# A hybrid encoder layer: the Hyena half of the output projection and the second norm, ordered by hand

## The chip, the cores and the metric

The kernel runs on one core of one Trainium2 chip. The metric is the time of one execution on the device in microseconds, the median of several runs; lower is better. The engines are PE (matmuls and transposes), DVE and POOL (element-wise work), ACT (element-wise work with functions, casts and copies) and SP, which here only issues DMAs; ACT can issue DMAs too.

## The reference

One encoder layer on 2048 positions of width 1024, in fp32. The left half of the projection's columns feeds an attention, the right half a Hyena operator (long convolutions by FFT, each followed by a gate); each half is RMS-normed by itself, both go through one output projection, and the sum with x is normed again ahead of a squared-ReLU MLP.

```python
def hyena_mixer(u, conv_w, conv_b, w1, ..., deltas, skip_d):
    uc = short_conv(u, conv_w, conv_b)
    v, x1, x2 = jnp.split(uc, HY_ORDER + 1, axis=-1)
    taps_f = hyena_filters_freq(seq_len, w1, b1, w2, b2, w3, b3, w4, freq, deltas)
    zz = v.astype(jnp.float32)
    gates = (x1, x2)
    for n in range(HY_ORDER):
        conv = fft_long_conv(zz, taps_f[:, n]) + skip_d[n].astype(jnp.float32) * zz
        zz = gates[n].astype(jnp.float32) * conv
    return zz.astype(u.dtype)

        mix = jnp.concatenate([rms_norm(att, attn_out_g[i]), rms_norm(hy, hy_out_g[i])], axis=-1)
        h = h + mix @ w_out[i]
        m = rms_norm(h, norm2_g[i])
        h = h + jnp.square(jax.nn.relu(m @ w_mlp_in[i])) @ w_mlp_out[i]
    return rms_norm(h, final_g)
```

## The kernel before, in words

**Precision.** An fp32 product is made of three matmuls (`mm3`, L162 to L164): both operands are split into a rounded part and a rest (hi and lo, type fp32r), and hi·hi, hi·lo and lo·hi are summed in one PSUM bank.

**Stages**, in microseconds from the start of the profiled span: the projection (0 to 230), attention with the Hyena inputs beside it (230 to 1226), the filters' transform (`filter_dft`, 1240 to 1415), the two convolutions (`conv` with o = 0 from 1420 and o = 1 from 1575), the rest of the output projection and the second norm (`mix`, 1719 to 1910), then the MLP's first and second matrix.

**Convolution's end.** The last loop of `conv` has 16 blocks of 32 channels. For each, PE transposes 8 tiles (bt, L1470), ACT copies them out of PSUM (b, L1471, two copies), PE makes 4 matmuls (yo, L1488), ACT copies one half of the result (odd, L1490), DVE adds and subtracts it (L1491, L1492), POOL multiplies by the gate (L1493), and SP writes the block to DRAM (z_d). The copies for a block stand ahead of the block before on PE and ACT (`turned(gb + 1)`).

**Attention half of the projection.** `att_part` is a generator: each step takes one chunk of 128 rows (three matmuls op of 128x512); eight steps make one tile of 128 positions, and h goes to h_d. Its steps are pumped between the steps of `filter_dft` and `conv` by the counts PUMP_F and PUMP_C; what is left runs at the start of `mix`.

**Mix.** For 16 tiles, in the order 0, 4, 1, 5, ... of each half: `hy_operands` loads 128 positions of z_d (mx), ACT casts hi (L622) and DVE subtracts lo (L623), ACT squares it (sq, L650), PE sums the squares over the channels (ss, L653), and DVE and ACT make the norm's factor (ar). `project` makes 24 matmuls (op) and DVE adds the result to h (L665). `normed` squares h on ACT with an accumulated sum (L730), makes the factor in small steps (r2, L112 to L119), and DVE writes m (L732). `turn` transposes the tile before (mt, L744, 8 transposes), and ACT scales the result into sa or sb (L746). After every second tile come four subtractions for the MLP's Strassen form (L705 to L707, L751), and `keep` splits seven operands of 128x512 (L759, L760), or in the second half writes them to mo_d. In `mlp_in`, two products run early ahead of the last tile's transposes (g), and the third (p = 6) needs sums of the weights' quarters (L697 to L699) and their split (wop, L819).

**What sets the order.** `filter_dft` and `conv` run under `in_order`: each engine takes its instructions as the code writes them. `mix` and the MLP are placed by the scheduler of the framework.

Of the kernel before, what the change touches and what calls it, by code (L numbers as in the profile page):

```python
# [45 lines left out]
def setup(tc, ctx, a):  # L46
# [19 lines left out]
    k.z_d = [k.dram.tile([HYW, SEQ], F32, name=f"z_d{i}") for i in range(2)]  # L66
# [537 lines left out]
def mix_setup(k, pool):  # L604
    nc, a = k.nc, k.a
    k.go = k.wa.tile([P, 8], F32, name="go")
    nc.scalar.dma_start(out=k.go[:, 0:4], in_=a["attn_out_g"][0].rearrange("(c p) -> p c", p=P),
                        allow_slow_non_contiguous=True)
    nc.scalar.dma_start(out=k.go[:, 4:8], in_=a["hy_out_g"][0].rearrange("(c p) -> p c", p=P),
                        allow_slow_non_contiguous=True)  # L610
    nc.vector.tensor_mul(out=k.go[:, 4:8], in0=k.go[:, 4:8], in1=k.norm[:])
    k.norm2 = k.wa.tile([P, 4], F32, name="norm2")
    aligned(k.wa, 64)
    nc.vector.tensor_mul(out=k.norm2[:], in0=k.norm[:], in1=k.norm[:])
    k.weights = mix_weights(k, pool, 0)
    next(k.weights)
# [28 lines left out]
def hy_operands(k, ps, t):  # L645
    nc = k.nc
    hx = k.wa.tile([P, 4, P], F32, name="mx", bufs=2)
    nc.sync.dma_start(out=hx[:], in_=k.z_d[1][:, t * P:(t + 1) * P].rearrange("(c p) t -> p c t", p=P))
    sq = k.wa.tile([P, 4, P], F32, name="sq")
    nc.scalar.activation(out=sq[:], in_=hx[:], func=AF.Square)  # L650
    sp = ps.get("s", "ss")
    for c in range(4):
        nc.tensor.matmul(sp[:, 0:1], sq[:, c], k.norm2[:, c:c + 1], start=c == 0, stop=c == 3)  # L653
    r = rstd_from_root(k, k.wa, sp[:, 0:1], QW, 1, "ar")
    return (*operand_parts(k, hx[:]), r)
# [57 lines left out]
def mix(k, mo, pool, ps, side, mlp):  # L713
# [7 lines left out]
    weights = mix_weights(k, mo, 1)  # L721
    next(weights)
    pump(side, 10 ** 6)
    hx = hy_operands(k, ps, tiles[0])
    *_, wo = weights

    def normed(h):
        m = mo.tile([P, DM], F32, name="m", tag="raw", bufs=NRAW)
        ssq = pool.tile([P, 1], F32, name="r2s", bufs=2)
        nc.scalar.activation(out=m[:], in_=h[:], func=AF.Square, accum_out=ssq[:])  # L730
        r2 = rstd_from_root(k, pool, ssq[:], DM, 1, "r2")
        nc.vector.tensor_scalar_mul(out=m[:], in0=h[:], scalar1=r2[:])  # L732
        return m

    def turn(half, i, s, m):
        if s == 0:
            k.sa = pool.tile([P, 2, 4, P], F32, name="sa", bufs=2)
        else:
            k.sb = pool.tile([P, 5, 4, P], F32, name="sb", bufs=1)
        b = k.sb if s else k.sa  # L740
        for c in range(2):
            tp = ps.get("s", "mt")
            for d in range(4):
                nc.tensor.transpose(tp[:, d * P:(d + 1) * P], m[:, (4 * c + d) * P:(4 * c + d + 1) * P], k.ident[:])  # L744
            for d in range(4):
                nc.scalar.mul(out=b[:, c, d], in_=tp[:, d * P:(d + 1) * P], mul=g2[:, 4 * c + d:4 * c + d + 1])  # L746
        if s:
            sa, sb = k.sa, k.sb
            engine = nc.gpsimd if half and i == 3 else nc.vector
            right_sums(engine, sb[:, 2], sb[:, 3], sb[:, 0], sa[:, 0], sb[:, 0], sb[:, 1])  # L750
            engine.tensor_sub(out=sb[:, 4], in0=sa[:, 1], in1=sb[:, 3])  # L751
            return half, slice(i * P, (i + 1) * P), [sa[:, 0], sa[:, 1]] + [sb[:, j] for j in range(5)]

    def keep(half, cs, ops):
        for j, x in enumerate(ops):
            if half:
                nc.sync.dma_start(out=k.mo_d[j, :, :, cs], in_=x)
                continue
            nc.scalar.copy(out=k.mh[j][:, :, cs], in_=x)  # L759
            (nc.gpsimd if j in MIX_POOL else nc.vector).tensor_sub(out=k.ml[j][:, :, cs], in0=x,  # L760
                                                                   in1=f32(k.mh[j][:, :, cs]))

    late, done = [], None
    for n, t in enumerate(tiles):
        h = pool.tile([P, DM], F32, name="h", bufs=2)
        nc.sync.dma_start(out=h[:], in_=k.h_d[t * P:(t + 1) * P, :])
        if n == NT - 2:
            next(mlp)
        cur = hx
        if n + 1 < NT:  # L770
            hx = hy_operands(k, ps, tiles[n + 1])
        for j in range(2):
            pump(project(k, ps, j, h[:, j * 512:(j + 1) * 512], wo, *cur), 10)
        nc.sync.dma_start(out=k.h2_d[t * P:(t + 1) * P, :], in_=h[:])
        due, done = done, None
        if len(late) == ML:
            done = turn(*late.pop(0))
        late.append((*order[n], normed(h)))
        if due:
            keep(*due)  # L780
    next(mlp)
    for x in late:
        done = turn(*x)
    keep(*done)


ML = 1
# [4 lines left out]
def mlp_in(k, mo, ps):  # L792
# [14 lines left out]
    def prepare(n, p):  # L807
        if p == 1:
            if n == 0:
                load(1)  # L810
# [361 lines left out]
def filter_taps(k, f1, ps):  # L1172
# [52 lines left out]
    nc.vector.reciprocal(out=k.norm[:], in_=k.norm[:])  # L1225

# [120 lines left out]
def filter_dft(k, g1, ps, side):  # L1347
# [6 lines left out]
    for o in range(2):  # L1354
# [13 lines left out]
        else:  # L1368
            k.feed.close()
            k.feed = Feed(k, "ux", a["dft_data"], [k.u_d[0:HYW], k.z_d[0]], (gps,), FEED_C, 16)  # L1370
# [22 lines left out]
PUMP_F = 6, 1  # L1393
FB = 6
FOLD_C = 8
PUMP_C = 4, 1, 3, 0


def conv(k, o, c1, ps, side):
    nc, a = k.nc, k.a  # L1400
    gate = blocks(k.u_d[(o + 1) * HYW:(o + 2) * HYW])
    dst = blocks(k.z_d[o])
# [72 lines left out]
    nc.sync.dma_start(out=d4[:], in_=a["idft"])  # L1475
    nxt = turned(0)
    for gb in range(16):
# [3 lines left out]
        pump(side, PUMP_C[3] * (gb % 2))  # L1481
# [3 lines left out]
        yo = ps.get("x", "yo")[:, 0].rearrange("p (q g m) -> p q g m", q=2, m=HF)  # L1485
        for q in range(2):
            for half in range(2):
                nc.tensor.matmul(yo[:, q], d4[:, q, half], cur[:, half, q], start=half == 0, stop=half == 1)  # L1488
        odd = c1.tile([P, 2, HYW], F32, name="odd", tag="t2", bufs=2)[:, 0, :4 * HF].rearrange("p (g m) -> p g m", m=HF)
# [4 lines left out]
        nc.sync.dma_start(out=dst[:, 4 * gb:4 * gb + 4], in_=gx)  # L1494
        if o == 0:
            k.feed.limit += 1
            k.feed.fill(gb >= FOLD_C)

# [94 lines left out]
def encoder_layer(tc, a):  # L1593
    with ExitStack() as ctx:
# [10 lines left out]
        with sbuf(k, "wa") as k.wa:  # L1605
            with sbuf(k, "hp") as hp, Banks(k, "ps3", {"s": 4}, {"x": 2}) as ps:
                side = att_part(k, hp, ps, list(range(NT)))
                with sbuf(k, "fd") as fd:
                    mix_setup(k, fd)
                    with in_order(tc):  # L1610
                        filter_dft(k, fd, ps, side)
                with sbuf(k, "cv") as cv, in_order(tc):
                    conv(k, 0, cv, ps, side)
                    conv(k, 1, cv, ps, side)
                k.feed.close()
                with sbuf(k, "mo") as mo:
                    mlp = mlp_in(k, mo, ps)
                    with sbuf(k, "mx") as mx:
                        mix(k, mo, mx, ps, side, mlp)
# [22 lines left out]
```

## Time and profile before

| | us |
|---|---|
| median of three runs | 3161.52 (3160.85 to 3162.79) |
| the profiled execution's own time | 3162.0 |
| its span, first to last instruction | 3160.1 |
| PE busy | 2997.1 (95%) |
| DVE busy | 2053.7 (65%) |
| POOL busy | 1683.2 (53%) |
| ACT busy | 1427.0 (45%) |
| mean granted TensorE clock | 0.974 of full speed |

A row of a window gives the length, then the busy time of each engine with its instructions, the granted clock of PE, the share of the DMA engines that is busy, and GB/s. A row of the waits names the waiting engine and instruction, what released it, the total, the number and the longest. In a timeline a row begins with its start and its duration; brackets give the idle time ahead of it.

### The profile page before, as it was taken

Reading aid. Unit: us, or ns where it says so; the run is one execution under the profiler, and the core shown is the slowest. Engines: PE = TensorE matmul, PEld = TensorE weight load, DVE = VectorE, ACT = ScalarE, POOL = GpSimd, SP = SyncE. Lnnn points to the kernel's source line nnn. Section 1 sums busy time; section 2 is a strip of 40 time slices with the busy share of each in tenths; the row PEclk is TensorE's granted clock in tenths of the full one; section 3 lists DMA queues with packets and bytes.
Section 4 is the critical chain, followed back from the end, with each engine's and each line's share of the span. In section 5 each row is a group of like instructions: output and inputs, shape, how many; then the busy total and the mean of one; then the engine's idle time right before and its main releaser. Section 6 shows DMA issues by size and latency. Waiting matters only on the chain.

```text
span 3160.1 us, 40370 instructions
## 1 busy us (share of the span) xinstructions
PE 2997.1 (95%) x13400; PEld 2258.8 (71%) x13400; DVE 2053.7 (65%) x3197; ACT 1427.0 (45%) x2641; POOL 1683.2 (53%) x1339
## 2 busy tenths in 40 slices
PE   7977999999999998999999888999999989999998
PEld 6754666666666666665757777888788878888887
DVE  7987776666665555777473667777977644454455
ACT  7865655555554444553434553333333233223333
POOL 3434777778778786335553116777877544250010
PEclk9988999999999999999999889999999999999999
DMA  7758344334423425776755455445544395433454
GB/s 224 222 153 235 113 128 143 110 108 136 140 101 121 153 77 173 262 253 192 206 160 181 134 183 182 152 150 176 201 165 155 120 326 173 133 116 128 143 184 153
DMA packets 477581, 518.67 MB, mean 164 GB/s; under 512 B 39604, under 2 KB 346292, under 8 KB 470332
## 3 DMA queue, kind: packets, MB, share of 16 engines
q1 hardware_dynamic: 472460, 512.11, 50.3%
q10 hardware_dynamic: 4912, 3.97, 0.5%
q8 instruction: 107, 1.75, 0.2%
q14 instruction: 102, 0.84, 0.1%
HBM read 321.99 MB, written 193.99 MB: 163 GB/s over the span
## 4 chain that ended last, share of the span: by engine, by line
PE 77%; DVE 6%; DMA 3%; POOL 2%; issue 2%; ACT 1%; SPq 0%; POOLq 0%; ACTq 0%; DVEq 0%
PE o L500 6%; PE y L163 6%; PE y L164 6%; PE y L162 6%; PE g L164 5%; PE g L163 5%; PE g L162 5%; PE st L479 4%; PE X L1335 3%; PE st L480 3%; PE sc L459 3%; PE uo L162 3%; PE uo L163 3%; PE uo L164 3%; PE yo L1488 2%
## 5 line engine op out<-in xcount | busy, mean ns | idle before, releaser
L487 POOL TENSOR_TENSOR sum<-sum,p 128x512 f32<-128x512 f32 x416 | 553.4, 1330 | 127.7 <-ACT p L482 101.7
L462 DVE TENSOR_REDUCE top<-sc 128x1 f32<-128x512 f32 x512 | 347.2, 686 | 260.2 <-PE sc L459 257.5
L482 ACT ACTIVATE p<-st 128x512 f32<-128x512 f32 x512 | 303.8, 598 | 310.4 <-PE st L480 295.4
L162 PE MATMUL g<-mh,wop 128*128 128x512 f32 x896 | 349.9, 391 | 6.8 <-ACT wop L819 6.8
L163 PE MATMUL g<-ml,wop 128*128 128x512 f32 x896 | 349.8, 390 | 4.2 <-DVE ml L830 4.2
L164 PE MATMUL g<-mh,wop 128*128 128x512 f32 x896 | 349.7, 390 | 0.4 <-DVE wop L820 0.4
L162 PE MATMUL y<-bh,ah 128*128 128x512 f32 x768 | 299.5, 390 | 7.8 <-ACT bh L987 7.8
L163 PE MATMUL y<-bh,ah 128*128 128x512 f32 x768 | 299.4, 390 | 0.9 <-DVE bh L988 0.9
L996 DVE TENSOR_TENSOR ah<-ar,ah 128x1024 fp32r<-128x1024 f32 x111 | 149.8, 1350 | 230.8 <-ACT ah L995 230.6
L164 PE MATMUL y<-bh,ah 128*128 128x512 f32 x768 | 299.3, 390 | 0.0
L995 ACT CAST ah<-ar 128x1024 fp32r<-128x1024 f32 x111 | 117.1, 1055 | 344.1 <-PE y L164 333.7
L500 PE MATMUL o<-p,vt 128*64 128x512 f32 x1024 | 234.9, 599 | 0.0
L459 PE MATMUL sc<-kt,q 128*128 128x512 f32 x512 | 208.0, 411 | 13.4 <-DVE top L462 11.3
L479 PE MATMUL st<-q,kt 128*128 128x512 f32 x512 | 214.7, 419 | 1.3 <-ACT p L482 1.2
L480 PE MATMUL st<-q,kt 128*128 128x512 f32 x512 | 203.1, 397 | 0.0
L162 PEld LDWEIGHTS g<-mh,wop 128*128 128x128 f32 x896 | 168.9, 189 | 42.1 <-ACT wop L819 7.0
L163 PEld LDWEIGHTS g<-ml,wop 128*128 128x128 f32 x896 | 168.8, 188 | 40.5 <-DVE ml L830 5.4
L164 PEld LDWEIGHTS g<-mh,wop 128*128 128x128 f32 x896 | 168.8, 188 | 36.2 <-DVE wop L820 1.1
L819 ACT CAST wop<-ws 128x512 fp32r<-128x512 f32 x128 | 79.2, 621 | 221.4 <-PE g L164 192.0
L162 PEld LDWEIGHTS y<-bh,ah 128*128 128x128 f32 x768 | 144.4, 188 | 38.4 <-ACT bh L987 8.4
L163 PEld LDWEIGHTS y<-bh,ah 128*128 128x128 f32 x768 | 144.5, 188 | 31.3 <-DVE bh L988 1.4
L164 PEld LDWEIGHTS y<-bh,ah 128*128 128x128 f32 x768 | 144.5, 188 | 29.9
(290 smaller groups left out, 7053.4 us busy)
## 6 DMA issues: line engine op xcount, KB each, us to landing
ar<-H_d SPq DMA_DIRECT2D x111, 512.0 KB, 3.9
uw<-uw_d SPq DMA_DIRECT2D x36, 1024.0 KB, 4.9
w1raw<-in_w_mlp_in SPq DMA_DIRECT2D x64, 512.0 KB, 4.1
H_d<-r SPq DMA_DIRECT2D x96, 256.0 KB, 2.2
H_d<-s SPq DMA_DIRECT2D x96, 256.0 KB, 2.0
F_d<-F SPq DMA_DIRECT2D x34, 512.0 KB, 2.8
F<-F_d SPq DMA_DIRECT2D x34, 512.0 KB, 4.1
aT<-aT_d SPq DMA_DIRECT2D x32, 512.0 KB, 6.1
```

Of the source, the lines that this page charges most:

```text
L162: mm(out, l_hi, r_hi, start=start, stop=False)
L163: mm(out, l_hi, r_lo, start=False, stop=False)
L164: mm(out, l_lo, r_hi, start=False, stop=stop)
L459: nc.tensor.matmul(s[:], u.q[:, h], kt[u.kv, b][0][:], start=True, stop=True)
L462: nc.vector.tensor_reduce(out=u.top[:, h, b:b + 1], in_=s[:], axis=AX.X, op=ALU.max, negate=True)
L479: nc.tensor.matmul(s[:], lo[:, c], u.q2[:].rearrange("p h t -> p (h t)"), start=True, stop=False)
L480: nc.tensor.matmul(s[:], hi[:, c], u.q[:].rearrange("p h t -> p (h t)"), start=False, stop=True)
L482: nc.scalar.activation(out=p[:], in_=s[:], func=AF.Exp)
L487: nc.gpsimd.tensor_add(out=u.sum[:], in0=u.p0[:] if j == 1 else u.sum[:], in1=p[:])
L500: nc.tensor.matmul(u.o[cols], vt[j // 8][:, j % 8, u.kv], p[:], start=j < 2, stop=j > 13)
L995: nc.scalar.copy(out=h[:, 0], in_=raw[:])
L996: nc.vector.tensor_sub(out=h[:, 1], in0=raw[:], in1=f32(h[:, 0]))
```

## The change

- **Attention half.** More steps are pumped (PUMP_F from 6, 1 to 6, 2; PUMP_C's last from 0 to 1, and in convolution 1 alone), and what is left at block 10 of convolution 1's last loop is run there. `mix` starts without any.
- **Hyena's norm.** While convolution 1's blocks leave, ACT squares them and PE sums them over channels by four matmuls with a selector sel (ssq_add); a table n2 of 512 factors is loaded for it by eight DMAs, and sel is made on DVE. The factor hr of all tiles is made once, at the end.
- **Hyena's parts.** hi and lo are made there too (POOL copies, DVE subtracts) and written to DRAM apart (zp_d); `hy_load` reads them. The weights' lower half wo is split there at blocks 11 to 14.
- **Mix by hand.** `mix` runs under `in_order`. Tile by tile: 24 products of one tile, then the transposes of the tile before; its norm runs under these products. The four subtractions and seven splits become a list of jobs, taken out one and five at a time.
- **Loads.** h has three buffers and is loaded two tiles ahead; the second load of the MLP's weights moves from p = 1 to p = 6.

```diff
+def hy_load(k, n, t):
+
+    first = n < 2
+    parts = []
+    for i in range(2):
+        name = "mx" if n % 3 == 2 else ("oh", "ol")[i]
+        p = k.wa.tile([P, 4, P], F32R, name=name, bufs=2)
+        src = k.zp_d[i, :, t * P:(t + 1) * P].rearrange("(c p) t -> p c t", p=P)
+        for c in range(4 if first else 1):
+            cs = slice(c, c + 1) if first else slice(0, 4)
+            k.nc.sync.dma_start(out=f32(p[:, cs]), in_=src[:, cs])
...
+    def added(u, j):
+        js = slice(j * 512, (j + 1) * 512)
+        nc.vector.scalar_tensor_tensor(out=u.h[:, js], in0=u.d[j][:], scalar=hr[:, u.t:u.t + 1], in1=u.h[:, js],
+                                       op0=ALU.mult, op1=ALU.add)
+
+    def squared(u, j):
+        js = slice(j * 512, (j + 1) * 512)
+        nc.scalar.activation(out=u.m[:, js], in_=u.h[:, js], func=AF.Square, scale=DM ** -0.5,
+                             accum_out=u.ssq[:, j:j + 1])
...
+    def normed(u):
+        nc.sync.dma_start(out=k.h2_d[u.t * P:(u.t + 1) * P, :], in_=u.h[:])
+        y, r, e = (pool.tile([P, 1], F32, name=f"r2{x}", bufs=2) for x in "yre")
+        nc.vector.tensor_scalar(out=y[:], in0=u.ssq[:, 0:1], scalar1=u.ssq[:, 1:2], scalar2=EPS,
+                                op0=ALU.add, op1=ALU.add)
+        nc.scalar.activation(out=e[:], in_=y[:], func=AF.Sqrt)
...
+        for j in range(2):
+            js = slice(j * 512, (j + 1) * 512)
+            nc.vector.tensor_scalar_mul(out=u.m[:, js], in0=u.h[:, js], scalar1=r[:])
...
+        for j in (4, 0, 5, 1, 6, 2, 3):
+            jobs.append(lambda j=j: keep(j))
...
+    for n in range(NT):
+        u = queue.pop(0)
+        if n + 2 < NT:
+            queue.append(load(n + 2))
...
+        if n == 0:
+            v = queue[0]
+            for w in (u, v):
+                for j in range(2):
+                    products(w, j, (0, 1, 2))
+            for j in range(2):
+                products(u, j, (3,))
...
+        if old:
+            added(old, 1)
+            squared(old, 1)
+            work(1)
+            normed(old)
+            if older:
+                taken(older)
+            turned(old)
+        room(u)
+        if n < NT - 1:
+            added(u, 0)
+            squared(u, 0)
+            work(5)
+        older, old = old, u
...
-PUMP_F = 6, 1
+PUMP_F = 6, 2
...
-PUMP_C = 4, 1, 3, 0
+PUMP_C = 4, 1, 3, 1
...
+def hy_sums(k, cz):
+
+    nc = k.nc
+    n2 = cz.tile([P, HYW // 8], F32, name="n2")
+    src = k.n2_d.rearrange("(g c) -> c g", c=8)
+    for c in range(8):
+        nc.scalar.dma_start(out=n2[c * NT:(c + 1) * NT], in_=src[c:c + 1].to_broadcast([NT, HYW // 8]),
+                            allow_slow_non_contiguous=True)
...
+    nc.vector.tensor_mul(out=sel[:], in0=mask[:].unsqueeze(1).to_broadcast([P, HYW // 8, NT]),
+                         in1=n2[:].unsqueeze(2).to_broadcast([P, HYW // 8, NT]))
...
+    def ssq_add(to, gb, z2):
+        for g in range(4):
+            nc.tensor.matmul(to[:, :NT], z2[:, g], sel[:, 4 * gb + g], start=g == 0, stop=g == 3)
+        nc.vector.tensor_add(out=k.hssq[:], in0=to[:, :NT], in1=k.hssq[:])
...
-        pump(side, PUMP_C[3] * (gb % 2))
+        if o and gb < 11:
+            pump(side, 10 ** 6 if gb == 10 else PUMP_C[3])
...
         nc.gpsimd.tensor_mul(out=gx, in0=y, in1=gx)
-        nc.sync.dma_start(out=dst[:, 4 * gb:4 * gb + 4], in_=gx)
...
+        nc.scalar.activation(out=y, in_=gx, func=AF.Square)
+        squares.append((gb, y))
+        hl = cz.tile([P, 2, 4, P], F32R, name="zp", bufs=2)
+        nc.gpsimd.tensor_copy(out=hl[:, 0], in_=gx)
+        nc.vector.tensor_sub(out=hl[:, 1], in0=gx, in1=f32(hl[:, 0]))
+        for i in range(2):
+            nc.sync.dma_start(out=dst[i][:, 4 * gb:4 * gb + 4], in_=f32(hl[:, i]))
+        if gb > 10:
+            k.wo1 = next(weights, None) or k.wo1
```

Three places show what the change does to the order. The first is ACT at the end of convolution 1, before: b are the copies out of PSUM for the next block, odd is the half of this block's result that DVE waits for.

```order
L1471 COPY b<-bt 128x512 x2
L1490 COPY odd<-yo 128x256
L1471 COPY b<-bt 128x512 x2
L1490 COPY odd<-yo 128x256
L1471 COPY b<-bt 128x512 x2
```

The same place after the change, from ACT's last copies of the inverse transform (L1532) to the second block; n is the table n2, L1616 is the square of a finished block.

```order
L1532 COPY A<-b 128x128x4 x20
L1487 DMA n_15338<-n_d 16x64x1 x8
L593 DMA oraw<-in_w_out 128x1024 x4
L1570 COPY b<-bt 128x512 x4
L1607 COPY odd<-yo 128x256
L1616 ACTIVATE both<-both 128x512
L1570 COPY b<-bt 128x512 x2
L1607 COPY odd<-yo 128x256
L1616 ACTIVATE both<-both 128x512
L1570 COPY b<-bt 128x512 x2
```

Between one block's odd and the next one's now stands the square of the first, with the copies behind it, and twelve DMA issues stand ahead of the first copies. The second place is DVE in `mix`'s first half after the change, from the step in which a pair of tiles is complete to the next; L805 to L808 are the four subtractions, L802 the rest of a split, L745 the addition to h, L760 to L769 the norm.

```order
L745 SCALAR_TENSOR_TENSOR h<-op,hr,h 128x512
L805 TENSOR_TENSOR sb<-sb,sa 128x512
L806 TENSOR_TENSOR sb<-sb 128x512
L807 TENSOR_TENSOR sb<-sb 128x512
L808 TENSOR_TENSOR sb<-sa,sb 128x512
L745 SCALAR_TENSOR_TENSOR h<-op,hr,h 128x512
L802 TENSOR_TENSOR ml_15983<-sa,mh_15976 128x4x128
L760 TENSOR_SCALAR r2y<-r2s 128x1
L763 RECIPROCAL r2r<-r2e 128x1
L764 TENSOR_TENSOR r2e<-r2r 128x1
```

The subtractions and splits of the pair before stand between the two halves of a tile's addition and ahead of its norm. The third place is ACT in the same step.

```order
L788 ACTIVATE sb<-mt,g_15974 128x128 x8
L750 ACTIVATE m,r2s<-h 128x512
L801 CAST mh_15980<-sb 128x4x128
L750 ACTIVATE m,r2s<-h 128x512
L801 CAST mh_15976<-sa 128x4x128
L762 ACTIVATE r2e<-r2y 128x1
L788 ACTIVATE sa<-mt,g_15974 128x128 x8
L750 ACTIVATE m,r2s<-h 128x512
L801 CAST mh_15981<-sb 128x4x128
L801 CAST mh_15977<-sa 128x4x128
```

The first cast of a pair (L801) reads what the first of the four subtractions on DVE wrote, and the square of the next half of h (L750) and the root for the norm (L762) queue behind it.

204 lines of the change are left out of this document (123 added, 81 removed).

## The prediction

> **What bounds the kernel now.** I read the chain that ended last first, then windows over the stretch that is rebuilt, then PE's waits in it.
>
> ```profile
> PE 77%; DVE 6%; DMA 3%; POOL 2%; issue 2%; ACT 1%; SPq 0%; POOLq 0%; ACTq 0%; DVEq 0%
> ```
>
> PE sets the end over three quarters of the span, so a stage is worth what PE idles or works in it. The windows: convolution 1's last loop, the attention half left over, `mix`'s first and second half, the step to the MLP's third product; then the filters' second loop and the rest of convolution 1.
>
> ```profile
> 1676.80:1718.80 42.00, 41.94 (x260) 37.66 (x258) 12.55 (x35) 24.09 (x51) 17.75 (x14) 1.00 0.55 160
> 1718.80:1747.00 28.20, 23.42 (x97) 18.38 (x96) 9.91 (x22) 5.02 (x9) 2.58 (x2) 0.88 0.71 225
> 1747.00:1862.00 115.00, 95.89 (x435) 80.01 (x434) 75.55 (x189) 63.72 (x169) 19.20 (x12) 0.85 0.39 127
> 1862.00:1903.10 41.10, 37.06 (x200) 30.70 (x199) 27.24 (x81) 23.74 (x72) 0.00 (x0) 1.00 0.89 271
> 1903.10:1916.60 13.50, 6.72 (x36) 5.45 (x34) 6.29 (x10) 5.45 (x19) 5.87 (x4) 0.84 0.72 210
> ...
> 1372.00:1415.00 43.00, 42.57 (x136) 24.94 (x137) 30.40 (x54) 22.17 (x31) 2.82 (x4) 1.00 0.82 297
> 1575.00:1676.80 101.80, 99.08 (x310) 58.53 (x311) 67.68 (x91) 36.45 (x79) 56.55 (x54) 0.97 0.53 165
> ```
>
> The first five make 239.8 us; everything of size in the change falls into them. The loop at the top is PE's (41.94 of 42.00); `mix`'s first half loses 19 us idle, and its clock is 0.85. PE's waits from 1718 to 1920:
>
> ```profile
> PE mt L744 <- DVE r2y L112: 17.7, 4, 4.4
> PE g L162 <- ACT wop L819: 6.8, 1, 6.8
> PE mt L744 <- DVE m L732: 4.7, 4, 2.0
> ```
>
> The transposes mt wait for the second norm, 22.4 us in all; the new order puts products over them. The idle time costs again, through the clock:
>
> ```profile
> 1781.84 1.19 PE L744 MATMUL mt<-ident,m 128*128 128x128 f32 x8 [4.40 <-DVE r2y L112]
> ...
> 1785.39 0.63 PE L164 MATMUL op<-wo,ol 128*128 128x512 f32 x1
> ...
> 1790.74 0.39 PE L164 MATMUL op<-wo,ol 128*128 128x512 f32 x1
> ```
>
> After 4.40 us of idling the matmuls last 0.63 us; five microseconds later 0.39 again, so some 0.2 us less each. The pace at full clock, from two early products (24 matmuls between the first row's end and the last), with the transposes and the old norm's sums:
>
> ```profile
> 1769.89 1.06 PE L744 MATMUL mt<-ident,m 128*128 128x128 f32 x8 [0.68 <-DVE m L732]
> 1770.80 0.95 PE L653 MATMUL ss<-norm,sq 128*128 128x1 f32 x8
> 1771.61 0.48 PE L162 MATMUL op<-wo,oh 128*128 128x512 f32 x1
> ...
> 1902.29 1.07 PE L744 MATMUL mt<-ident,m 128*128 128x128 f32 x8 [1.96 <-DVE m L732]
> 1903.11 0.48 PE L162 MATMUL g<-mh,wop 128*128 128x512 f32 x1
> ...
> 1908.69 1.03 PE L744 MATMUL mt<-ident,m 128*128 128x128 f32 x8
> ```
>
> 1903.11 to 1908.69 is 5.58 us, 0.2325 a matmul; eight transposes take 0.91 and 0.82, so 0.87; ss takes 0.81.
>
> **Part 1, attention half.** The second window's matmuls are 29 steps of three; 29 x 3 x 0.2325 = 20.2 us. They go to places where PE has no room (42.57 of 43.00, 99.08 of 101.80), so they are paid in full there, with some transposes 20.5. The 28.2 us go. Their DMAs (512 KB of h in and out a tile) join a window at 297 GB/s and share 0.82, in which each step also lengthens the loop by 0.7 us; I take nothing for them, bound 3.
>
> **Part 2, convolution 1's last loop.** One block of before:
>
> ```profile
> 1696.67 0.37 ACT L1490 COPY odd<-yo 128x256 f32<-128x256 f32 x1 [1.08 <-issue]
> 1697.11 1.07 ACT L1471 COPY b<-bt 128x512 f32<-128x512 f32 x2
> 1697.13 0.42 DVE L1491 TENSOR_TENSOR both<-yo,odd 128x256 f32<-128x256 f32 x1 [1.83 <-POOL both L1493]
> ...
> 1698.02 1.27 POOL L1493 TENSOR_TENSOR both<-both 128x512 f32<-128x512 f32 x1 [1.32 <-DVE both L1492]
> ...
> 1699.27 0.37 ACT L1490 COPY odd<-yo 128x256 f32<-128x256 f32 x1 [1.08 <-issue]
> ```
>
> The period is 2.60 us, and ACT runs ahead: its copies follow odd at once. In the new order the square of this block stands ahead of those copies. So odd (1696.67) to POOL's end (1699.29) is 2.62 us, then the square, then the copies, then the next odd: a closed loop. A square of 128x512 is 0.64 us, in the groups of `mix`:
>
> ```profile
> L760 POOL TENSOR_TENSOR ml<-sb,mh 128x512 fp32r<-128x512 f32 x12 | 19.2, 1626 | 109.1 <-DVE are L117 55.3 <-DMA mx<-z_d 53.8
> ...
> L650 ACT ACTIVATE sq<-mx 128x512 f32<-128x512 f32 x15 | 9.7, 643 | 0.9 <-PE ss L653 0.9
> ...
> L598 DVE SCALAR_TENSOR_TENSOR wo<-oraw,go,wo 128x1024 fp32r<-128x1024 f32 x4 | 5.1, 1278 | 0.9 <-ACT wo L597 0.9
> ...
> L705 DVE TENSOR_TENSOR sb<-sb,sa 128x512 f32<-128x512 f32 x7 | 4.8, 692 | 1.5 <-ACT sb L746 1.4
> ...
> L597 ACT ACTIVATE wo<-oraw,go 128x1024 fp32r<-128x1024 f32 x3 | 3.4, 1137 | 0.0
> ```
>
> 2.62 + 0.64 + 1.07 + 0.1 for the hand-over is 4.4 us; PE's own work, 2.60 and 0.8 for the selector (by ss, which is four such matmuls), hides in it. With the wo split (1.14) four blocks take 5.5. Fifteen periods: 11 x 4.4 + 4 x 5.5 = 70.4 us, where before took 39. DVE and POOL have a branch of similar length: additions, gate, POOL's copy, the rest 0.69, the sums 0.2. The copy has no row; by L760 it is at most 1.63 us, at least nothing, and I take 1.0. Only at the upper end does the branch (4.9 us) outlast the loop, which would add 7 us. I take 4.4.
>
> Ahead of the first block DVE makes sel, which waits for the eight loads of n2: 8192 separate values of 4 bytes. The trace shows no such load behind a matmul stage. Its nearest are g (1024 values) and cb, which queues behind cw (18 KB, issued 0.4 us before; together 6144 values):
>
> ```profile
> g<-in_norm_g ACTq DMA_DIRECT2D x2, 4.0 KB, 2.4
> ```
>
> ```profile
> cw<-in_hy_conv_w SPq DMA_DIRECT2D x1, 18.0 KB
> ...
> cb<-in_hy_conv_b SPq DMA_DIRECT2D x1, 6.0 KB, 11.4
> ```
>
> By g the eight take 2.4 us (side by side) to 19 us (one behind the other); by cw and cb 1.9 ns a value, 15.7 us. I take 12, between. With issue 0.7 and sel 1.28 (as L598, DVE at 128x1024), the first block's sum starts at 14 us instead of 4.5, bounds 4.5 and 21. The last block's then starts at 14 + 70.4 = 84.4 us (before: 42).
>
> The Trainium skill, page "DMA: Bandwidth & Descriptors", section "Rules for kernel authors", says that a strided last dimension lowers to one descriptor per element, which speaks against this load; the queue of cw and cb agrees in kind. From the same page's 10.5 ns per packet ("Bandwidth", measured), 512 packets an engine would be 5.4 us, an estimate, and the sum 7 us lower.
>
> **Part 3, into mix.** From the last sum: DVE 0.75, POOL 1.4 and its copy 1.0, rest 0.7, a write and a load.
>
> ```profile
> z_d<-both SPq DMA_DIRECT2D x16, 256.0 KB, 3.2
> mx<-z_d SPq DMA_DIRECT2D x16, 256.0 KB, 3.6
> ```
>
> That is 10.7 us; the 36 products of chunks 0 to 2 (8.4 us) lie within. Chunk 3 starts at 95.1 us. The factor hr of all tiles is ready long before; its small steps hide there.
>
> **Part 4, mix.** PE from there: 12 + 14 x 24 = 348 matmuls x 0.2325 = 80.9; 16 x 8 transposes at 0.87 per eight 13.9; two early products 5.6; 100.4 us together (the ss matmuls are gone). The first transposes follow chunk 3 of two tiles, and of their norm's 5 us only six matmuls of tile 1 (1.4) lie beside it: 3 to 4 us, I take 3. After the idle start a dozen matmuls take 0.2 us more each: 2.3. The step into the third product stays, since the last transposes still come behind the two early products:
>
> ```profile
> 1915.83 1.66 ACT L819 CAST wop<-ws 128x512 fp32r<-128x512 f32 x3 [3.81 <-DVE ws L698]
> ```
>
> ACT's scaling, the weights' sums, wop: all remains, 6.8 us of waiting. The weights' second load, now behind p = 6, costs nothing: five products of 2.8 us lie ahead of its use, and its 512 KB, twice an mx (3.6), land in some 4 to 7; without that cover it would be as much.
>
> The first half's norm is not free. The steps' durations:
>
> ```profile
> L665 DVE SCALAR_TENSOR_TENSOR h<-op,ar,h 128x512 f32<-128x512 f32 x33 | 24.5, 744 | 29.1 <-PE op L164 24.3 <-DMA h<-h_d 4.4 <-DMA h<-in_x 0.4
> ...
> L759 ACT CAST mh<-sb 128x512 fp32r<-128x512 f32 x20 | 11.3, 650 | 0.0
> L732 DVE TENSOR_SCALAR m<-h,r 128x1024 f32<-128x1024 f32 x15 | 11.2, 750 | 0.3
> ```
>
> Transposes and products take 6.45 us a tile; from the end of a tile's products to its transposes lie about 5 us of addition, square, factor and m, hidden when the queues are empty. But the jobs stand in them. In the step after a pair DVE goes: addition 0.74, four subtractions 2.75, addition 0.74, square on ACT 0.85, cast 0.6, rest 0.69, factor 1.2 (six small ones), m 0.8, hand-overs 0.4: 8.8 us. The other step, with five casts for the subtractions, takes 7.9. 16.7 against 12.9 a pair, three and a half pairs: 13 us, bounds 0 (queues overlap after all) and 18. In the second half the jobs are transfers: window 1862 ran 271 GB/s at share 0.89, so some 304 at full share. A pair then moves 4.9 MB (hi and lo double the loads), 16 us against 12.9 of PE; loads run two tiles ahead. I take 2 us, bounds 0 and 8.
>
> 100.4 + 3 + 2.3 + 6.8 + 13 + 2 = 127.5.
>
> **Sum.** 20.5 + 95.1 + 127.5 = 243.1 us against 239.8: +3.3. The profiled execution took 3162.0 against a median of 3161.5, 0.5 us apart; from either it comes to **3165 us**. About 50 us of waits, ss matmuls and slow clock are removed, and the loop gives about as many back. A difference of 0.2%, 6.3 us, is what a measurement can tell from no change: 3155.2 to 3167.8.
>
> **Rivals.** (a) Faster, 0.33: n2 lands early (2.4 to 5 us) and the jobs overlap with the products. For it: ACT and DVE have only 63.72 and 75.55 of 115 us to do there. It takes off 7 to 9 and 5 to 13: 3143 to 3153. The loop of 4.4 us remains: that is the order.
> (b) Slower, 0.26: n2 comes at cb's rate or slower, with ACT, whose copies stand behind those issues, held as SP was for 8.66 us there:
>
> ```profile
> 242.32 8.66 SPq L337 DMA_DIRECT2D cb<-in_hy_conv_b  x1
> ```
>
> Above 16 us of landing it adds 4 to 7, and the second half, bound by DMA, 3 to 6 more: 3172 to 3184.
> (c) The clock drops in the loop, 0.05: PE would idle 1 us in each 4.4. After the 1.96 us of idling ahead of 1902.29 the matmuls keep their 0.2325 us, so I think it stays. If it fell to half, 3.4 us of work would be 6.2 a block: 3190 or more. The Trainium skill, "TensorE: Matmul & The Clock Gate", section "A second HAM failure mode: psum-queue depth-cycling", says that micro-idling between groups can make the clock swing; no wait of this trace shows it.
> (d) The order does not do what it says, the waits on the norm return under new names, 0.04: near 3161.
>
> **Chances.** My forecast has 0.32, own range 3154 to 3174: 0.04 of it faster, 0.18 same, 0.10 slower. With (a) faster, (b) and (c) slower, (d) same: faster 0.37, same 0.22, slower 0.41. The range takes in (a) and (b): 3142 to 3184.
>
> **What would show it.** In the new profile the loop's odd copies lie 4.3 to 4.5 us apart, ended by the square; a spacing of 3.4 refutes part 2. The first addition is released by sel some 14 us after the first bt. No att or ss matmuls in `mix`; the windows of filter and convolution grow by 20 us. In the first half the transposes come every 7.9 and 8.8 us; at 6.45, (a) is right. The clock reads 1.00 from the second tile on. What would make me wrong most is a landing of n2 far from 12 us, or the jobs' price.

## The result, and the profile after

The changed kernel takes 3191.53 us (3184.39 to 3193.71, four runs) against 3161.18 us (3160.70 to 3162.79, four runs): a ratio of 1.0091, 95% interval 1.0074 to 1.0109, 0.9% slower. The forecast was 3165 us, with a range of 3142 to 3184 that took in two of the rivals; the result lies above it.

The chain that ended last in the profile after, and the windows of the rebuilt stretch: the loop of convolution 1 with its start, the step into `mix`, first half, second half, the step to the MLP's third product, and last the loop again without its start:

```profile
PE 74%; DVE 6%; DMA 4%; issue 2%; ACT 2%; POOL 2%; SPq 1%; ACTq 0%; POOLq 0%; DVEq 0%
```

```profile
1700.20:1785.30 85.10, 66.54 (x398) 55.82 (x399) 29.27 (x65) 34.48 (x67) 28.21 (x30) 0.94 0.60 162
1785.30:1792.80 7.50, 4.47 (x24) 3.43 (x22) 2.66 (x10) 0.85 (x2) 1.91 (x2) 0.88 0.37 82
1792.80:1896.70 103.90, 87.56 (x364) 69.90 (x365) 71.61 (x145) 57.67 (x178) 18.84 (x12) 0.86 0.69 217
1896.70:1916.00 19.30, 19.30 (x98) 16.06 (x97) 11.25 (x30) 8.47 (x29) 0.00 (x0) 1.00 0.93 288
1916.00:1940.00 24.00, 9.41 (x42) 7.17 (x40) 11.81 (x20) 10.17 (x34) 5.81 (x4) 0.74 0.74 217
...
1716.00:1785.00 69.00, 60.11 (x372) 50.54 (x371) 28.02 (x63) 31.84 (x63) 28.21 (x30) 1.00 0.58 166
```

The loop, full of PE before, now leaves it idle for 18.6 of 85.1 us; the first half still has 16 us of idling and a clock of 0.86; and a stretch at the end, 24 us long, has 14.6 us of idling where before there were 6.8 in 13.5. PE's waits from 1700 to 1940 name them:

```profile
PE yo L1603 <- ACT b L1570: 17.3, 13, 9.7
PE mt L775 <- DVE m L769: 16.3, 7, 3.2
PE g L164 <- ACT wop L899: 14.6, 2, 11.4
```

The 22.4 us for the norm became 16.3, the 6.8 for wop became 14.6, and the 17.3 of the loop are new. Cut at events that both timelines show, the two profiled executions differ as follows; the forecast's terms are put at the same cuts. "First matmul (fs)" is that of the filters' transform, bt are the transposes and odd the copies of the loop's blocks.

| stretch, us | before | forecast | after |
|---|---|---|---|
| start to the filters' first matmul (fs) | 1227.1 | 1227.1 | 1235.4 |
| to the loop's first bt | 449.7 | 470.2 | 464.9 |
| to the first odd | 4.2 | 13.6 | 15.5 |
| first odd to the last | 38.2 | 70.4 | 69.2 |
| to the first transposes of `mix` | 42.5 | 19.2 | 15.4 |
| first to last transposes of `mix` | 147.0 | 111.8 | 127.2 |
| to the third product of the MLP | 7.8 | 7.7 | 12.4 |
| to the end | 1243.6 | 1243.6 | 1250.6 |

The rows add up to the spans, 3160.1 and 3190.6, and to 3163.6 for the forecast. The loop, the largest cost in the forecast, came as worked out. Four rows took longer than the forecast: the first (+8.3), the sixth (+15.4), the seventh (+4.7), the last (+7.0). The first and the last lie where the change was thought to do nothing. Each column is one execution. Between executions of kernels whose code is alike there, the first row varies by 6 us and the second by 3, so that for these two the waits tell more than the rows.

### The profile page after: what moved, and what is told of

It is laid out like the page before. It is cut to its first block, busy times and chain, and to the rows that moved or that the text cites. A ratio compares the mean times of both kernels' runs of the same rounds, so it can differ in the third digit from the quotient of the medians.

```text
span 3190.6 us, 40450 instructions
## 1 busy us (share of the span) xinstructions
PE 3001.4 (94%) x13400; PEld 2258.6 (71%) x13400; DVE 2054.0 (64%) x3157; ACT 1418.0 (44%) x2642; POOL 1694.0 (53%) x1355
## 4 chain that ended last, share of the span: by engine, by line
PE 74%; DVE 6%; DMA 4%; issue 2%; ACT 2%; POOL 2%; SPq 1%; ACTq 0%; POOLq 0%; DVEq 0%
PE y L164 6%; PE o L502 6%; PE y L165 6%; PE y L166 6%; PE g L166 6%; PE g L165 5%; PE g L164 5%; PE st L481 4%; PE X L1417 4%; PE st L482 3%; PE sc L461 3%; PE uo L164 3%; PE uo L165 3%; PE uo L166 3%; PE b L1545 2%
## 5 line engine op out<-in xcount | busy, mean ns | idle before, releaser
L164 PE MATMUL g<-mh,wop 128*128 128x512 f32 x896 | 350.9, 392 | 14.6 <-ACT wop L899 14.6
L164 PE MATMUL y<-bh,ah 128*128 128x512 f32 x768 | 299.8, 391 | 15.7 <-ACT bh L1067 15.7
L164 PEld LDWEIGHTS g<-mh,wop 128*128 128x128 f32 x896 | 169.5, 189 | 50.6 <-ACT wop L899 15.1
```

The source lines that it names most:

```text
L164: mm(out, l_hi, r_hi, start=start, stop=False)
```

## The experiments

Each is made from the changed kernel if not said otherwise, and the kernel before ran beside each. The first four take one suspected cost away.

**Addresses.** The first wait of the MLP's second matrix, before and after:

```profile
2530.10 0.39 ACTq L974 DMA_DIRECT2D ar<-H_d  x1
...
2534.97 1.14 ACT L1017 CAST ah<-ar 128x512 fp32r<-128x512 f32 x2 [4.30 <-DMA ar<-H_d]
```

```profile
2559.21 0.44 ACTq L1054 DMA_DIRECT2D ar<-H_d  x1
...
2565.98 1.14 ACT L1097 CAST ah<-ar 128x512 fp32r<-128x512 f32 x2 [12.32 <-DMA ar<-H_d]
```

Before, ACT issued the first load of the next stage 5.3 us ahead of the end of POOL's last instruction (2534.10 to 2535.36); after, 0.9 us behind it (2557.09 to 2558.35). The code there is the same. But the tiles of `hp` are closed ahead of `mix` now, so everything opened later lies 5888 bytes lower, and the first buffer ar (at byte 214272 of a partition in both) covers tiles r, which the MLP uses until its end, where before it covered other tiles.

```diff
                     with sbuf(k, "mi") as k.mi:
+                        aligned(k.mi, 5888)
                         pump(mlp)
```

> The changed kernel with 5888 bytes of unused space ahead of the MLP's tiles, so that these lie again where they lay before the change. Theory: the first wait of the MLP's second matrix (15.7 us for bh against 7.8 before) comes from the addresses alone: with the attention's tiles closed ahead of mix, the MLP's tiles moved down and the first activation buffer of the next stage (ar) now lies on tiles that POOL reads until its last instruction. Then that wait falls to about 7.8 us and the time by 7 to 9 us (3183 from 3191). Rival: the wait is a transfer that came late by itself, or the spread between runs; then the wait stays near 15 and the time within 2 us of the changed kernel's.

Measured: 3182.5 us (3178.4 to 3189.3), 1.0071 of the kernel before (1.0050 to 1.0092). PE's wait for bh, 7.8 us before the change and 15.7 after, was back near the first:

```profile
PE y L164 <- ACT bh L1067: 8.3, 2, 7.1
```

From the third product to the end it took 1243.9 us, against 1243.6 before the change and 1250.6 after. The interval of the ratio overlaps that of the changed kernel, so the row decides, not the time: in all seven profiles of the changed kernel and its edits without the padding it is 1249.5 to 1251.9 us, in all five with it 1242.7 to 1245.2. So the addresses are the whole of the last row.

**The loads of n2.** ACT's and DVE's start of the loop in the changed kernel:

```profile
1699.59 8.92 ACTq L1487 DMA_DIRECT2D n<-n_d  x8
...
1708.55 2.61 ACTq L593 DMA_DIRECT2D oraw<-in_w_out  x4
1711.20 2.05 ACT L1570 COPY b<-bt 128x512 f32<-128x512 f32 x4 [11.03 <-DMA n<-n_d]
...
1711.99 1.23 DVE L1492 TENSOR_TENSOR sel<-mask,n 128x1024 f32<-128x1024 f32 x1 [13.10 <-DMA n<-n_d]
...
1715.70 0.37 ACT L1607 COPY odd<-yo 128x256 f32<-128x256 f32 x1 [2.45 <-issue]
1716.11 0.43 DVE L1608 TENSOR_TENSOR both<-yo,odd 128x256 f32<-128x256 f32 x1 [2.87 <-ACT odd L1607]
```

The issue alone holds ACT 8.92 us, with the weights' loads behind it until 1711.16, and only then come the copies b. The table is there 12.4 us after its first issue, and DVE is done with sel at 1713.22. The first addition, at 1716.11, does not wait for sel but for ACT's odd.

```diff
-    src = k.n2_d.rearrange("(g c) -> c g", c=8)
+    src = k.n2t_d
...
+    nc.sync.dma_start(out=k.n2t_d[:], in_=k.n2_d.rearrange("(g c) -> c g", c=8), allow_slow_non_contiguous=True)
```

> The changed kernel with the table n2 turned once in DRAM at the start of the filters' transform, so that the eight loads read rows of 256 bytes instead of single values. Theory: the 15.9 us from the loop's first transposes to its first sum are the 8192 separate values (ACT held 8.9 us by their issue, DVE by the last landing); it falls to 5 to 7 us and the time by 8 to 11 us. Rival: the loop's start waits for something behind it (the weights' loads that ACT issues next, or the gate's blocks), or later work absorbs the gain: less than 4 us.

Measured: 3186.9 us (3179.6 to 3188.0), 1.0078 (1.0060 to 1.0096). The first odd came 9.3 us after the first bt instead of 15.5; the rest is ACT's twelve issues, 5.6 us long. By the medians the time fell by 4.7 us, less than the 8 to 11 that were expected and more than the rival's; the intervals overlap. The separate values cost 6.1 us of the loop's start, and ACT's issues most of the other half (the run without any, below, has 3.8).

**The jobs of the second half.** ACT and PE at the end of `mix`, after:

```profile
1917.51 2.18 ACT L788 ACTIVATE sb<-mt,g 128x128 f32<-128x128 f32 x8 [5.79 <-DMA mo_d<-sb]
...
1932.83 2.18 ACT L788 ACTIVATE sb<-mt,g 128x128 f32<-128x128 f32 x8 [6.67 <-DMA mo_d<-sb]
```

```profile
1920.24 0.50 PE L164 MATMUL g<-mh,wop 128*128 128x512 f32 x1 [3.23 <-ACT wop L899]
...
1939.96 0.79 PE L164 MATMUL g<-mh,wop 128*128 128x512 f32 x1 [11.36 <-ACT wop L899]
```

There is one buffer sb, and the writes of the pair before still read it, since the jobs issue them over three steps. The early products g and the third product wait for the splits wop, which stand behind this scaling in ACT's order.

```diff
             added(u, 0)
             squared(u, 0)
-            work(5)
+        work(99 if n > 10 else 5)
```

> The changed kernel with the jobs of the second half (four subtractions and seven writes of a pair) issued in one step, right when the pair is complete, instead of over three steps. Theory: at the end of mix ACT's scaling of sb waits for the writes of the pair before (one buffer), 5.8 and 6.7 us, and PE's early products and the third product behind it, 3.2 and 11.4 us with slow clock after each. With the writes earlier both waits shrink: 3.2 to about 0, 11.4 to about 7 and the time by 6 to 10 us. Rival: the transfers are bound by bandwidth there (share 0.93), so that the writes land as late as before whatever the step: less than 3 us.

Measured: 3179.5 us (3176.5 to 3181.7), 1.0056 (1.0038 to 1.0074). The wait of 3.23 is gone, 11.4 became 8.1; the sixth row fell to 119.9, the seventh to 9.1, together 10.6 us, and the medians by 12.0. The writes were late by their place in the order, not by the bandwidth.

**The closed loop.** One block, after:

```profile
1719.78 0.38 ACT L1607 COPY odd<-yo 128x256 f32<-128x256 f32 x1
...
1721.09 1.27 POOL L1610 TENSOR_TENSOR both<-both 128x512 f32<-128x512 f32 x1 [2.14 <-issue]
...
1722.39 0.63 ACT L1616 ACTIVATE both<-both 128x512 f32<-128x512 f32 x1 [2.22 <-POOL both L1610]
...
1722.92 1.06 ACT L1570 COPY b<-bt 128x512 f32<-128x512 f32 x2
...
1723.93 0.37 ACT L1607 COPY odd<-yo 128x256 f32<-128x256 f32 x1
```

Odd, gate product, square, copies, odd: 4.15 us, and ACT is idle for 2.22 of them.

```diff
+        if o and gb:
+            square()
         nc.vector.tensor_add(out=y[:, :, :HF], in0=yo[:, 0], in1=odd)
         nc.vector.tensor_sub(out=y[:, :, ::-1][:, :, :HF], in0=yo[:, 0], in1=odd)
+        if o and gb:
+            rest()
```

Here `square` and `rest` (lo and the two writes) are those of the block before; PE's sums, left out above, take the square that is then at hand.

> The changed kernel with the square and the rest (lo) of each block in convolution 1's last loop one block later on ACT and DVE, so that neither stands between a block's gate product and the next block's copies. Theory: the loop's period of 4.14 us (5.3 to 5.9 with the weights' split) is the closed loop odd, sums, gate product, square, copies; opened, PE's 3.4 us remain, 15 periods fall from 69 to about 52 us and the time by 13 to 17 us. Rival: another loop of nearly the same length (POOL's two instructions, or the gate's transfers) takes its place: a period of 3.8 or more and less than 8 us.

Measured: 3175.2 us (3173.5 to 3176.8), 1.0046 (1.0031 to 1.0060). The period is 3.45 us, 4.15 in the last four, and the first to the last odd take 53.9 us instead of 69.2. The time fell by 16.3 us, within what was expected. The loop was the order of the engines' queues, not work.

**Part 1 alone**, in the kernel before, by one number:

```diff
-PUMP_F = 6, 1
+PUMP_F = 6, 2
```

> The kernel before with only the pumping counts of the changed one in the filters' transform (two steps a turn instead of one), so that mix starts without attention steps; all else as before. Theory: the 28.2 us stretch with the left-over steps goes and 20 to 21 us come back in the filters' transform, where PE is as full: 5 to 9 us faster than the kernel before. Rival: the moved steps' transfers make the filters' loops wait, or convolution 1's end is late for mix without the left-over steps to cover it (a wait on the load of z_d's last block): within 3 us of the kernel before, or slower.

Measured: 3167.9 us (3163.1 to 3171.3), 1.0012 (1.0002 to 1.0023): not faster, as the rival had it. The filters and convolutions grew by 15.1 us, and `mix` begins with a wait that the left-over steps had covered:

```profile
PE ss L653 <- ACT sq L650: 15.3, 2, 13.2
```

That is the last block's write and load (ACT's sq waits for mx). Steps that look movable were the cover of a round trip through DRAM. In the changed kernel its early products of chunks 0 to 2 take that place.

**The four edits together.**

> The changed kernel with the four single edits together (addresses, n2 turned in DRAM, the second half's jobs at once, square and rest one block later). If the four costs are separate their sum is 6.7 + 6.1 + 10.6 + 15.4 = 39 us by the traces: 3150 to 3156, faster than the kernel before by 4 to 10. Rival: they hide one another (an earlier loop end meets the load of the first tiles, the early writes meet the bandwidth): 3160 or more.

Measured: 3153.8 us (3151.0 to 3157.9), 0.9976 (0.9965 to 0.9987). The four costs add up, within a few us (38 us by the medians, 39 expected), and without them the change is faster than the kernel before.

**The first half's jobs.** PE after a wait there, in the changed kernel:

```profile
1849.82 1.94 PE L775 MATMUL mt<-ident,m 128*128 128x128 f32 x8 [3.17 <-DVE m L769]
...
1852.84 0.63 PE L164 MATMUL op<-wo,mx 128*128 128x512 f32 x1
```

After this wait the transposes and some of the next matmuls run at half the pace. The spacing of the transposes was 9.65, 9.07, 9.81, 9.21 ... us: 18.8 a pair, not the forecast's 16.7. But the slow pace is not what sets it. The transposes wait for DVE's m, and from 1830 to 1887 DVE has no wait on PE, only on ACT: it goes its own round, from m to m in 9.05 and 9.8 us. In that round some of its instructions of 128x512 take twice as long as others of the same form:

```profile
1851.43 0.69 DVE L806 TENSOR_TENSOR sb<-sb 128x512 f32<-128x512 f32 x1
1852.04 0.68 DVE L807 TENSOR_TENSOR sb<-sb 128x512 f32<-128x512 f32 x1
1852.07 1.78 POOL L802 TENSOR_TENSOR ml<-sb,mh 128x512 fp32r<-128x512 f32 x1 [6.75 <-ACT mh L801]
1852.64 1.76 DVE L808 TENSOR_TENSOR sb<-sa,sb 128x512 f32<-128x512 f32 x1
...
1856.37 0.69 DVE L802 TENSOR_TENSOR ml<-sa,mh 128x512 fp32r<-128x512 f32 x1 [1.30 <-ACT mh L801]
...
1861.17 3.00 POOL L802 TENSOR_TENSOR ml<-sb,mh 128x512 fp32r<-128x512 f32 x2 [7.32 <-ACT mh L801]
1861.65 1.38 DVE L802 TENSOR_TENSOR ml<-sa,mh 128x512 fp32r<-128x512 f32 x1 [1.87 <-ACT mh L801]
1862.95 2.38 DVE L802 TENSOR_TENSOR ml<-sb,mh 128x512 fp32r<-128x512 f32 x2
```

Those that begin while POOL is at work (L808, two of the rests L802) take 1.4 to 1.8 us and end behind POOL's instruction; those with POOL idle, or begun just ahead of it (L807), take 0.68 to 0.69. It is so in all four pairs.

```diff
+        if n <= 10:
+            work(7 if older and order[older.n][2] else 99)
         room(u)
         if n < NT - 1:
             added(u, 0)
             squared(u, 0)
-            work(5)
+            work(5 if n > 10 else 0)
```

The fourth subtraction and one more rest go to POOL with it, the splits are taken in another order, and the single job ahead of the norm is left out for these tiles.

> The changed kernel with the jobs of the first half put ahead of a tile's first addition instead of behind it (seven and four a step), and one subtraction and one more rest on POOL. Theory: the 9.65 and 9.07 us between transposes in the first half are the jobs in DVE's and ACT's queues between a tile's products and its norm, and the slow clock that follows a wait of 3 us; spacings fall to 6.5 to 7.5 us, six of them, and the time by 10 to 17 us. Rival: the queues are full (DVE's and ACT's work a pair is near 13 us), so that the jobs delay the norm wherever they stand: spacings of 8.5 or more and less than 5 us.

Measured: 3180.5 us (3177.3 to 3186.4), 1.0057 (1.0036 to 1.0077). The time fell by 11.0 us, within what was expected, but the spacings only went to 8.65 and 8.05, 16.7 a pair: between the expectation and its rival. DVE's rests show why (the groups of the first half, before the change, then this kernel):

```profile
L760 DVE TENSOR_TENSOR ml<-sa,mh 128x512 fp32r<-128x512 f32 x8 | 5.2, 684 | 0.0
```

```profile
L802 DVE TENSOR_TENSOR ml<-sa,mh 128x512 fp32r<-128x512 f32 x8 | 13.9, 1781 | 0.0
```

All eight rests of sa now begin while POOL is at work and take 1.78 us instead of 0.68. (In the changed kernel the groups' means are 1.03 for sa's and 1.23 for sb's, since half of each ran without POOL.) Here too DVE has no wait on PE between these transposes.

**All of it, and no issues by ACT.** n2 is loaded at the filters' transform and the weights' lower half by SP.

```diff
+    k.n2 = k.wa.tile([P, HYW // 8], F32, name="n2")
+    for c in range(8):
+        nc.sync.dma_start(out=k.n2[c * NT:(c + 1) * NT], in_=k.n2t_d[c:c + 1].to_broadcast([NT, HYW // 8]))
...
-        (nc.scalar if part else nc.sync).dma_start(out=raw[:], in_=a["w_out"][0, r0:r0 + P, :])
+        nc.sync.dma_start(out=raw[:], in_=a["w_out"][0, r0:r0 + P, :])
```

> All of these edits together, and n2 loaded at the filters' transform and the weights' lower half by SP, so that no transfer is issued by ACT ahead of the loop. If the costs are separate: the four single edits 39 us, the first half's jobs 10 to 17, the loop's start 4 to 5 more: 3132 to 3142, faster than the kernel before by 18 to 28 us. Rival: once the first half runs at PE's pace the loads of h and of the parts bind there, and the gain of the jobs shrinks to less than half: 3145 to 3150.

Measured: 3140.3 us (3137.7 to 3144.9), 0.9925 (0.9904 to 0.9945). The first odd came 3.8 us after the first bt.

**The first row.** What PE waited for from 928 to 1028, in the attention, was POOL before and after, but 4.1 and 14.3 us:

```profile
PE of L511 <- POOL ob L505: 4.1, 1, 4.1
```

```profile
PE of L513 <- POOL ob L507: 14.3, 1, 14.3
```

The instruction that PE waits for stood in POOL's order behind one that waits for the filters' taps. SP's rows there, after:

```profile
974.34 0.36 SPq L1307 DMA_DIRECT2D n_d<-total  x1
...
976.66 18.83 SPq L1366 DMA_DIRECT2D x<-taps_d  x10
```

Before, these ten issues took 9.34 us. New is the write of n2, 512 values of 4 bytes. Two edits tell the number of writes from the queue that they stand in: rows of 16 bytes (the first diff, with a transfer inside DRAM into the final order later), or another queue (the second).

```diff
-    nc.sync.dma_start(out=k.n2_d.rearrange("(c p) -> p c", p=P), in_=total[:, 0], ...)
+    nc.sync.dma_start(out=k.n2p_d[:], in_=total[:, 0])
...
+    nc.sync.dma_start(out=k.n2_d.rearrange("(c p) -> p c", p=P), in_=k.n2p_d[:], allow_slow_non_contiguous=True)
```

```diff
-    nc.sync.dma_start(out=k.n2_d.rearrange("(c p) -> p c", p=P), in_=total[:, 0], ...)
+    nc.scalar.dma_start(out=k.n2_d.rearrange("(c p) -> p c", p=P), in_=total[:, 0], ...)
```

> The changed kernel with the 512 factors of n2 written during attention as 128 rows of 16 bytes, and put into their final order by a transfer inside DRAM at the start of the filters' transform. Theory: the 512 separate writes of 4 bytes into one 2 KB region, put on SP's queue ahead of the ten loads of the filters' taps, are what makes those loads land 14 us late instead of 4, so that POOL, and PE behind it, wait 14.3 us in the attention (4.1 before the change); with rows that wait is back at 4 to 5 us, the filters' transform starts 8 to 10 us earlier and the time falls by 7 to 11 us. Rival: the loads are late for another reason (their place in the order, the addresses in DRAM): the wait stays at 14.

> The changed kernel with the same 512 writes of 4 bytes of n2, issued by ACT instead of SP. If it is the order within SP's queue (the taps' loads stand behind the writes) the wait of 14.3 us in the attention falls to 4 to 6 us here too. If the writes hold the shared engines whoever issues them, it stays above 10 us.

Measured: with rows 3184.0 us (3179.4 to 3188.1), 1.0070 (1.0055 to 1.0085), a wait of 6.2 us; from ACT 3192.0 (3190.5 to 3193.5), 1.0095 (1.0080 to 1.0111), 12.6 us:

```profile
PE of L514 <- POOL ob L508: 6.2, 1, 6.2
```

```profile
PE of L513 <- POOL ob L507: 12.6, 1, 12.6
```

So it is the separate writes, whoever issues them. The wait is 12.6 to 14.5 us in all nine profiles of kernels with them, 6.0 to 6.2 in the three with rows, 4.1 and 3.9 in the two without a table. The row itself says less: with this wait taken off it is anywhere from 1217 to 1225 us in these fourteen profiles, so that the +8.3 of the table is 10.2 of the wait less 1.9 of other differences.

**All of it, with rows.**

> All edits of the earlier combined kernel and the writes of n2 in rows. If the attention's 10 us are separate from the rest: 3128 to 3134, faster than the kernel before by 27 to 33 us. Rival: the filters' transform starts earlier but waits for its tables and taps: 3136 or more.

Measured: 3133.1 us (3129.7 to 3137.4), 0.9906 (0.9889 to 0.9922), the lowest median of all. Its first half still has mostly 7.8 to 8.9 us between transposes; the last run, an edit to this kernel, asked whether POOL's share does that.

```diff
-        jobs.append(lambda: nc.gpsimd.tensor_sub(out=sb[:, 4], in0=sa[:, 1], in1=sb[:, 3]))
+        jobs.append(lambda: engine.tensor_sub(out=sb[:, 4], in0=sa[:, 1], in1=sb[:, 3]))
...
-MIX_POOL = 3, 4, 5, 6
+MIX_POOL = 4, 5, 6
```

> The second combined kernel with the fourth subtraction and one rest back from POOL to DVE. In the second combined kernel two of DVE's rests take 1.78 us each instead of 0.69, and POOL is busy in just that stretch. Theory: the two engines hold each other up there, and that is what still keeps the first half at 16.7 us a pair; with less of POOL's work beside them the rests fall below 1 us, the spacing of 8.7 to 8.9 to 7.5 to 8, and the time by 2 to 4 us against the second combined kernel (3129 to 3131). Rival: DVE's two extra instructions (1.4 us a pair) cost as much as they free: within 1.5 us of it, or slower.

Measured: 3134.0 us (3132.7 to 3141.6), 0.9923 (0.9911 to 0.9935): no gain, spacings of 8.7 and 9.2. Three of DVE's four rests a pair still began while POOL was at work and took 1.4 to 1.8 us (the groups' means are 1.23 and 1.57). So the edit did not do what it was made for, and how much of the round a POOL that is out of the way would give back stays open.

## Why the prediction was wrong

The forecast was too low by 37 us in five rows of the table and too high by 10 us in three, 27 together.

- **"Everything of size in the change falls into them"**, said of the five windows, failed. 15 of the 37 us lie outside: 8.3 in the attention (the separate writes of n2, a line of the diff that was not priced) and 7.0 at the MLP's end (addresses). Edits in rows and in addresses took back most of the one wait and all of the other.
- **Part 1** was forecast at 20.5 us of cost in the filters and convolutions; it was 15.2. PE's busy time there grew by 19.7 us, as forecast, but 4.5 of them filled time in which it had been idle, where the prediction took the added work to be paid in full. (Other profiles of kernels with the same counts have 11.7 to 18.8 us.) That the 28.2 us "go" was right only with the early products behind them: alone the step gains nothing.
- **Part 2** held for the loop: 4.15 us a block for 4.4, 69.2 us for 70.4. "A closed loop" is shown by opening it. At the loop's start the number was near, the first odd at 15.5 us for 13.6, but part of that is luck. The table's 12.4 us came close to the 12 chosen between 2.4 and 19, yet "the first addition is released by sel" failed: sel was done 2.9 us before that addition, and what the addition waited for was ACT, held by its own issues until 1711.16, then its copies and PE's products. Only rival (b) had named ACT there.
- The Trainium skill's page "DMA: Bandwidth & Descriptors", section "Rules for kernel authors", warned of one descriptor per element, and both places agree: the load of n2 (6.1 us of the loop's start gone with contiguous rows) and its write (the wait at 6.2 us instead of 14.3 with rows). The estimate of 5.4 us from its figure per packet was too low; the trace's own bounds (2.4 to 19) held the value.
- **Part 3** was 3.2 us too careful to the first product of chunk 3 (7.5 for 10.7 us).
- **Part 4, the first half**, was mis-sized: 13 us over PE's pace, measured 24 (eight spacings that exceed 6.45 by 2.6 to 3.4). The step that failed is "rest 0.69" and "four subtractions 2.75". Two rests and the fourth subtraction of each pair began while POOL was at work on its own rests, and took 1.4 to 1.8 us each, by the rows 2.9 us a pair more. DVE's round was 9.05 and 9.8 us instead of 8.8 and 7.9, 2.2 us a pair more than forecast, which makes 21 us in seven spacings.
- **"The clock reads 1.00 from the second tile on"** failed too: waits of 3.0 to 3.2 us were each followed by half the pace. For most of the half this cost next to nothing, since the transposes would have waited for DVE anyway; the eighth spacing, 2.75 us over PE's pace, is the slow clock after the last wait. The Trainium skill's page "TensorE: Matmul & The Clock Gate", section "Why this matters for your kernels", asks for no idle gaps over some 3 us; here shorter ones did harm as well, and the runs draw no line. The prediction took from one wait of 1.96 us that the clock stays. The same wait in the kernel with part 1 alone was followed by transposes at near half the pace, while one of 3.29 us in the kernel whose n2 is written by ACT was not:

```profile
1902.34 1.74 PE L744 MATMUL mt<-ident,m 128*128 128x128 f32 x8 [1.96 <-DVE m L732]
```

```profile
1884.03 1.06 PE L775 MATMUL mt<-ident,m 128*128 128x128 f32 x8 [3.29 <-DVE m L769]
```

- **"The step into the third product stays"** failed: 14.6 us of waiting instead of 6.8, with some 2 us of slow clock. The jobs, which replaced an order chosen by the scheduler, issued the writes of sb so late that the next use of sb waited for them. The 2 us set for the second half's transfers were never needed as such; its inner tiles ran at 6.4 us.
- **The rivals.** (b) had the right sign, and ACT was held by its issues as it said (8.92 us). But the landing of 12.4 us is not the "above 16" that it priced, and its second mechanism, bandwidth, was not what happened. (c), the slow clock in the loop, had the nearest time (3190 or more) and the wrong mechanism: from 1716 to 1785 the clock read 1.00.

## What to carry to other kernels

Price every line of a diff, the small transfers first: 512 writes of 4 bytes cost about 8 us here, in a stage whose own code was left alone. When a queue is ordered by hand, follow each engine's rows around one period and look for a circle through two queues; moving one row by a period opens it. When instructions are priced from rows, see what the other engines did beside those rows and will do beside the new ones. When pools are closed earlier, compare the addresses of what comes later, since a buffer that slides onto a late reader adds a wait in code that nobody touched.

## What was not expected of the hardware

- 512 separate writes of 4 bytes held up ten loads behind them by about 9 us, from SP's queue and from ACT's alike; as 128 rows of 16 bytes by about 2.
- A DVE instruction of two operands in SBUF that begins while POOL works on one of its own: up to 1.8 us instead of 0.68, ending behind POOL's; one that begins 0.03 us ahead of POOL's keeps its 0.68. The Trainium skill's page "SBUF — State Buffer", section "SBUF: two separate sides", tells of a port pair that DVE, with two operands in SBUF, and POOL lock against each other for a whole instruction. The rows agree, case by case within one kernel; no run here took POOL away altogether.
- Waits of 2 to 3.3 us ahead of PE's transposes were followed by half the pace in some cases and by the full pace in others, one of 1.96 us in the same code both ways.
